# Decoder layer on one core: the down projection as seven 2x2 block products instead of eight

## The chip, the cores and the metric

One Trainium2 chip, of which the program uses a single core. The metric is the device time of one execution in microseconds (us), as the median of several runs. The profile is one further execution, taken by the hardware profiler.

## The reference

One inference step of a decoder layer for 1024 prompt tokens and 8 sample tokens, 1032 in all, in 32-bit floats. Sparse attention, a gated delta rule and a cross-attention over memory come first; the change leaves their code alone. It concerns the last line of the layer, a SwiGLU feed-forward of width 2816 on a model width of 1024:

```python
hf = rmsnorm(x, ffn_norm_g)
x = x + (jax.nn.silu(hf @ w_gate) * (hf @ w_up)) @ w_down
```

## The kernel before

Activations stand transposed: 128 features on the partitions, tokens along the free dimension. So the hidden activations are 22 row blocks of 128 features by 1032 tokens, and the residual `xT` is 8 blocks of 128 by 1032. The tokens are split into a first half of 512 (`HN`) and a second of 520 (the 8 sample tokens stand at its end).

Every product is made to nearly full precision from three matmuls in the faster format (`three`, L1775, and `proj`, L129). Each operand is split into a rounded part `h` and a rest `l`, and TensorE sums h*h, h*l and l*h. For weights `split_w` (L121) does this: a cast on ScalarE (L125) makes `wh`, a subtraction on GpSimd (L126) makes `wl`, with two buffers for each. For activations `split` (L142) does it with a cast on ScalarE (L143) and a subtraction on VectorE (L144).

**Gate and up units.** Eleven calls of `unit_product` (L1812) make two row blocks of the hidden activations each. They already use a 2x2 block scheme: sums of weight blocks (`S`, L1836), split into `sh` and `sl` (L1841, L1842) with seven buffers each, against sums of activations (`T2` to `T4`), in pieces of 260 tokens. One of the four result blocks, the first row block for the first token half, is made by `early` and `first` (L1784, L1801) before the units. In the unit the results are in `uu` (three buffers in all) and `s1`; gate results pass through SiLU on ScalarE, GpSimd multiplies gate and up (L1900), and SP's queue stores the products into a scratch tensor `scrF` in DRAM (L1901).

**Down projection.** `stage_down` (L1940) fetches hidden row blocks from `scrF` (`fetch`, L1934: load `af`, then `split`) in three lots of 8, 7 and 7 blocks, and reloads the residual from `scrT`. `down` (L1903) goes over the 8 output blocks of 128: load the weights (`load_w`, L113), split them, and for each group of tokens (512, 256 and 264, `GROUPS2`) make the product into a PSUM bank `pd`, which VectorE adds to `xT` (L1913). The first lot is done for the group of 512 first and then for the other two groups. With the last lot `store_y` (L1917) transposes each finished output block on TensorE (bank `py`) and stores it.

The order of the instructions on each engine and queue is set by the framework's list scheduler, from the order in the program as priority and from its own estimate of times; on the chip each engine and queue then takes its list in order. Tiles of one tag share a fixed number of buffers, and a tile waits until one is free. Unit tiles (`unit`, tag `u`) have five buffers in this stage.

Of the kernel before, what the change touches and what calls it, by code (L numbers as in the profile page):

```python
# [6 lines left out]
F32 = mybir.dt.float32  # L7
FR = mybir.dt.float32r
BF = mybir.dt.bfloat16
I32 = mybir.dt.int32  # L10
# [3 lines left out]
OP = mybir.AluOpType  # L14
# [25 lines left out]
class Kernel:  # L40
# [111 lines left out]

    def consts(self):
        nc, c = self.nc, self.c
        jp = c.tile([128, 128], I32, name="jp")
# [1645 lines left out]
    def first(self, u, kind, s1, p, sg):  # L1801

        V = self.nc.vector
        if kind == "gate":
            V.tensor_add(sg[:, 0], s1, p)
            self.silu(sg[:, 0], sg[:, 0])
        else:
            V.tensor_add(sg[:, 1], s1, p)  # L1808
            self.nc.gpsimd.tensor_mul(sg[:, 1], sg[:, 0], sg[:, 1])
            self.nc.sync.dma_start(self.scrF[2 * u, :, 0:HN], sg[:, 1])  # L1810

    def unit_product(self, u):  # L1812

        nc, V = self.nc, self.nc.vector
        w = HN + NS
        halves = (slice(0, w // 2), slice(w // 2, w))
# [4 lines left out]
        sg = {}  # L1821
        for kind in ("gate", "up"):
            raw = []
# [22 lines left out]
            t2 = total(t1, a11)  # L1846
            t4 = total(a12, t2)
# [44 lines left out]
            c = [u1, u2[:, :HN], s1]  # L1892
            if kind == "gate":
                for x in c:
                    self.silu(x, x)
                sg["c"] = c
            else:
                f = 2 * u
                for x, y, dst in zip(c, sg["c"], (self.scrF[f, :, HN:], self.scrF[f + 1, :, 0:HN], self.scrF[f + 1, :, HN:])):
                    nc.gpsimd.tensor_mul(x, x, y)  # L1900
                    nc.sync.dma_start(dst, x)  # L1901

    def down(self, f0, acts, groups, last=False):  # L1903
        nc, V = self.nc, self.nc.vector
        kt = len(acts)
        for o in range(KD):
            wh, wl = self.load_w(self.i["w_down"][0][128 * f0:128 * (f0 + kt), 128 * o:128 * o + 128], kt, 128)
            for g in groups:
                g0, n = self.G[g]
                p = self.bank("g", "pd")  # L1910
                self.proj(wh, wl, 0, 128, g, p, kt=kt, act=lambda k: [x[:, g0:g0 + n] for x in acts[k]])
                x = self.xT[:, o, g0:g0 + n]
                V.tensor_add(x, x, p[:, :n])  # L1913
            if last:
                self.store_y(o)

    def store_y(self, o):  # L1917
        nc = self.nc
        cs = slice(128 * o, 128 * o + 128)
        for half in range(2):  # L1920
            p = self.bank("g", "py")
            for t in range(4):
                c = 128 * (4 * half + t)
                self.tr(p[:, 128 * t:128 * t + 128], self.xT[:, o, c:c + 128], 128)
            y = self.unit("y", [128, 4, 128])
            (nc.vector.tensor_copy if half else nc.scalar.copy)(y, p.rearrange("p (t c) -> p t c", c=128))
            nc.sync.dma_start(self.o["y_prompt"][0, 512 * half:512 * half + 512, cs].rearrange("(t p) c -> p t c", p=128), y)
        p = self.bank("g", "py")
        self.tr(p[:NS, :128], self.xT[:, o, T:NT], 128)
        y = self.unit("y8", [NS, 128])  # L1930
        nc.scalar.copy(y, p[:NS, :128])
        nc.scalar.dma_start(self.o["y_sample"].rearrange("b o d -> (b o) d")[:, cs], y)

    def fetch(self, f, h, l, s):  # L1934

        a = self.unit("af")[:, :s.stop - s.start]
        self.nc.sync.dma_start(a, self.scrF[f, :, s])
        self.split(a, h[:, s], l[:, s])

    def stage_down(self, after_units):  # L1940

        acts = [(self.AH[:, k], self.AL[:, k]) for k in range(KD)]
        n1, n2, n = slice(0, HN), slice(HN, NT), slice(0, NT)
        for f in range(8):
            self.fetch(f, *acts[f], n1)
        after_units()
        for o in range(KD):
            self.nc.sync.dma_start(self.xT[:, o, n1], self.scrT[:, o, n1])  # L1948
        for f in range(8):
            self.fetch(f, *acts[f], n2)  # L1950
        self.down(0, acts, (0,))
        for o in range(KD):
            self.nc.sync.dma_start(self.xT[:, o, n2], self.scrT[:, o, n2])
        self.down(0, acts, (1, 2))
        more = [[self.du.tile([128, UW], FR, name="d" + x, tag="d")[:, :NT] for x in "hl"] for _ in range(7)]
        for f in range(8, 15):
            self.fetch(f, *more[f - 8], n)
        self.down(8, more, (0, 1, 2))
        for f in range(15, 22):
            self.fetch(f, *acts[f - 15], n)  # L1960
        self.down(15, acts[:7], (0, 1, 2), True)


    def build(self):
        tc, nc = self.tc, self.nc
        P = tc.alloc_tile_pool
# [5 lines left out]
        self.AH = self.act.tile([128, KD, NT], FR, name="AH")  # L1972
        self.AL = self.act.tile([128, KD, NT], FR, name="AL")
# [55 lines left out]
        self.scrT, self.scrF = self.dr.tile([128, KD, NT], F32, name="scrT"), self.dr.tile([22, 128, NT], F32, name="scrF")  # L2029
# [8 lines left out]
        m = lambda name, shape, dt=FR: self.mkp.tile(shape, dt, name=name)  # L2038
# [13 lines left out]
        def after_units():  # L2052
            for p in (self.tp, self.gw, self.gv):
                p.release()
            self.keep = P(name="keepD", bufs=1)
            self.xT = self.keep.tile([128, KD, NT], F32, name="xT")
            self.du = P(name="du", bufs=14)

        self.stage_down(after_units)
        for p in (self.wp, self.du, self.keep, self.u, self.act, self.c, self.dr, self.ps):  # L2060
            p.release()

    def sample_gen(self):
# [33 lines left out]
```

## Time and profile before

| | |
|---|---|
| median of 3 runs | 1780.9 us (1780.2 to 1784.61) |
| the profiled execution's own time | 1789.59 us |
| its span, first to last instruction | 1787.4 us |
| mean granted clock of TensorE | 0.952 |
| gate and up units in the span | about 1193 to 1513 us |
| down stage in the span | about 1513 us to the end |

TensorE's clock is given as a share of its full 2.4 GHz. Matmuls are pipelined: the duration of one is longer than the distance to the next, so the cost of a matmul is read from the distance of starts. Idle time of an engine is put down to what ended the wait.

### The profile page before, as it was taken

To read this page: it belongs to the slowest core of one execution; us is meant where nothing else is said; L and a number is where in the kernel's file an instruction comes from. 1 tells how busy PE (TensorE), PEld (TensorE's weight loads), DVE (VectorE), ACT (ScalarE), POOL (GpSimd) and SP (SyncE) were. 2 spreads that over 40 slices of the span, in tenths; PEclk is the share of its full clock that TensorE was granted. 3 is DMA by queue.
4 is the path that set the end of the run, shared out by engine and by line. 5 is a ranking of instruction groups with operands and counts; after the bars stand their busy time and mean duration, and the time that the engine had idled before them with its cause. 6 is when DMAs were issued, how large, how long until landed. Compare 5 with 4: busy or idle time off the path is not lost. (4 is left out here: it accounts for less than half of the span.)

```text
span 1787.4 us, 31531 instructions
## 1 busy us (share of the span) xinstructions
PE 1634.5 (91%) x11316; PEld 1442.3 (81%) x11316; DVE 1106.3 (62%) x2913; ACT 880.8 (49%) x2069; POOL 827.7 (46%) x791
## 2 busy tenths in 40 slices
PE   6999988768859999989998899879999999899998
PEld 5989877768747777768896578669999999599998
DVE  7699996999979777762355523775556666313111
ACT  5568879964546666664565564432222323212111
POOL 1277663573147133225553436765656566342210
PEclk9999998879979899979998999989999999999999
DMA  4134354324242324256322244553444444922132
GB/s 156 46 91 130 118 145 125 119 90 134 85 121 63 82 72 122 78 156 184 89 83 59 79 140 148 190 160 101 137 125 126 130 131 132 313 82 86 42 90 58
DMA packets 268630, 206.44 MB, mean 115 GB/s; under 512 B 31397, under 2 KB 240506, under 8 KB 268338
## 3 DMA queue, kind: packets, MB, share of 16 engines
q1 hardware_dynamic: 249674, 175.34, 32.6%
q0 software_dynamic: 4864, 14.69, 2.9%
q10 hardware_dynamic: 13936, 14.40, 2.3%
q8 instruction: 89, 1.46, 0.3%
q14 instruction: 67, 0.55, 0.1%
HBM read 152.01 MB, written 52.47 MB: 114 GB/s over the span
## 5 line engine op out<-in xcount | busy, mean ns | idle before, releaser
L126 POOL TENSOR_TENSOR wl<-raw,wh 128x1024 fp32r<-128x1024 f32 (+2 forms) x107 | 255.3, 2387 | 401.8 <-ACT wh L125 329.0
L48 PE MATMUL pm<-AH,wh 128*128 128x384 f32 (+7 forms) x792 | 269.8, 341 | 4.6 <-ACT y L111 4.0
L48 PE MATMUL pm<-AH,wl 128*128 128x384 f32 (+7 forms) x792 | 263.0, 332 | 0.1
L48 PE MATMUL pm<-AL,wh 128*128 128x384 f32 (+7 forms) x792 | 262.7, 332 | 0.1
L125 ACT CAST wh<-raw 128x1024 fp32r<-128x1024 f32 (+2 forms) x107 | 110.0, 1029 | 255.5 <-PE pd L48 172.4
L48 PEld LDWEIGHTS pm<-AH,wh 128*128 128x128 f32 (+1 forms) x792 | 154.0, 195 | 12.0 <-ACT y L111 4.6
L1842 POOL TENSOR_TENSOR sl<-S,sh 128x512 fp32r<-128x512 f32 x88 | 119.7, 1371 | 89.6 <-ACT sh L1841 86.9
L48 PEld LDWEIGHTS pm<-AL,wh 128*128 128x128 f32 (+1 forms) x792 | 154.0, 194 | 6.7 <-issue 0.8
L48 PEld LDWEIGHTS pm<-AH,wl 128*128 128x128 f32 (+1 forms) x792 | 152.9, 193 | 5.1 <-issue 0.7
L1913 DVE TENSOR_TENSOR xT<-xT,pd 128x256 f32<-128x256 f32 (+2 forms) x72 | 36.8, 512 | 190.5 <-PE pd L48 190.4
L1841 ACT CAST sh<-S 128x512 fp32r<-128x512 f32 x88 | 53.3, 619 | 183.5 <-DVE S L1836 170.6
L48 PE MATMUL pd<-AH,wh 128*128 128x512 f32 (+2 forms) x360 | 116.3, 325 | 5.1 <-ACT wh L125 5.1
L48 PE MATMUL pd<-AH,wl 128*128 128x512 f32 (+2 forms) x360 | 115.4, 322 | 3.7 <-POOL wl L126 3.7
L48 PE MATMUL pd<-AL,wh 128*128 128x512 f32 (+2 forms) x360 | 115.1, 321 | 0.0
L1836 DVE TENSOR_TENSOR S<-raw 128x512 f32<-128x512 f32 x44 | 54.8, 1246 | 92.0 <-DMA raw<-in_w_gate 38.0
L48 PE MATMUL p<-AL,sh 128*128 128x260 f32 x352 | 99.7, 283 | 0.0
L48 PE MATMUL p<-AH,sh 128*128 128x260 f32 x352 | 99.6, 283 | 0.0
L48 PE MATMUL p<-AH,sl 128*128 128x260 f32 x352 | 99.3, 283 | 0.0
L48 PE MATMUL pg<-AH,wh 128*128 128x512 f32 x176 | 73.3, 419 | 14.6 <-DVE sg L1808 7.5
L1866 DVE TENSOR_TENSOR uu<-uu,p 128x260 f32<-128x260 f32 x176 | 71.9, 420 | 16.4 <-PE p L48 14.7
L48 PEld LDWEIGHTS pd<-AH,wh 128*128 128x128 f32 x360 | 68.1, 189 | 11.9 <-ACT wh L125 6.8
L48 PEld LDWEIGHTS pd<-AH,wl 128*128 128x128 f32 x360 | 67.9, 189 | 10.6 <-POOL wl L126 5.3
(703 smaller groups left out, 5153.8 us busy)
## 6 DMA issues: line engine op xcount, KB each, us to landing
raw<-in_w_gate SPq DMA_DIRECT2D x33, 512.0 KB
raw<-in_w_up SPq DMA_DIRECT2D x33, 512.0 KB
raw<-in_w_in SPq DMA_DIRECT2D x24, 512.0 KB
raw<-in_w_out SPq DMA_DIRECT2D x16, 512.0 KB
raw<-in_w_down SPq DMA_DIRECT2D x16, 512.0 KB
af<-scrF SPq DMA_DIRECT2D x14, 516.0 KB
raw<-in_w_down SPq DMA_DIRECT2D x16, 448.0 KB
scrG<-y ACTq DMA_DIRECT2D x32, 192.0 KB
```

Of the source, the lines that this page charges most:

```text
L48: return self.nc.tensor.matmul(out, lhsT, rhs, start=start, stop=stop)
L125: self.nc.scalar.copy(wh, raw)
L126: self.nc.gpsimd.tensor_sub(wl, raw, f32(wh))
L1836: op(t, x, y)
L1841: nc.scalar.copy(h, x)
L1842: nc.gpsimd.tensor_sub(l, x, f32(h))
L1866: V.tensor_add(out[:, c], x[:, c], p[:, :w // 2])
L1913: V.tensor_add(x, x, p[:, :n])
```

## The change

The hidden activations are now four blocks: b11 and b12 (even row blocks, first and second token half), b21 and b22 (odd row blocks). The down weights are four blocks A11, A12, A21, A22: output half by even or odd row blocks, each 512 outputs by 11 row blocks. Instead of eight block products `stage_down` makes seven, of these weights and operands, in this order: A11 with b11 (operand 0), A22 with operand 4, S1 with 1, S2 with 2, S4 with 5, S3 with 3, A12 with b21 (operand 6). Only A11's and A12's are 512 tokens wide; the others have 520, in two pieces of 260.

The operands' sums are made in the units by a new function `down_blocks` and stored in a scratch tensor `scrD`. The weights' sums stay in one buffer `S`, which each product turns into the next: S1 = A22 + A21, S2 = S1 - A11, S4 = A12 - S2, S3 = A11 - A21 (this one loads two blocks). Weights come in pieces of six and five row blocks per output block. A sum `U` collects what goes into several results. Operands of the next product are fetched two per step during the current one, into the other half of `AH` and `AL` or into six buffers `du`; the residual is reloaded piecemeal in the first three products. `store_y` now stores one token half at a time. Other edits: `AH` and `AL` are 1040 instead of 1032 wide, and the index tile `jp` moves to the pool of unit tiles. The core of the diff:

```diff
-            self.nc.sync.dma_start(self.scrF[2 * u, :, 0:HN], sg[:, 1])
+            self.nc.sync.dma_start(self.scrD[0, u, :, :HN], sg[:, 1])
...
             if kind == "gate":
...
+                b11 = self.unit("b11", [128, HN])
+                nc.sync.dma_start(b11, self.scrD[0, u, :, :HN])
             else:
-                f = 2 * u
-                for x, y, dst in zip(c, sg["c"], (self.scrF[f, :, HN:], self.scrF[f + 1, :, 0:HN], self.scrF[f + 1, :, HN:])):
-                    nc.gpsimd.tensor_mul(x, x, y)
-                    nc.sync.dma_start(dst, x)
+                self.down_blocks(u, b11, (u1, u2, s1), sg["c"])
+    def down_blocks(self, u, b11, up, gate):
+        nc, G, V = self.nc, self.nc.gpsimd, self.nc.vector
+        (b12, b21, b22), (t3, t4, t2) = up, gate
+        store = lambda j, x: nc.sync.dma_start(self.scrD[j, u, :, :x.shape[-1]], x)
+        G.tensor_mul(b12, b12, t3)
+        G.tensor_mul(b22, b22, t2)
+        G.tensor_mul(b21[:, :HN], b21[:, :HN], t4[:, :HN])
+        store(5, b22)
+        store(6, b21[:, :HN])
+        V.tensor_sub(t3, b22, b12)
+        store(3, t3)
+        V.tensor_sub(b12[:, :HN], b12[:, :HN], b11)
+        store(1, b12)
+        G.tensor_sub(t2, b22, b12)
+        store(2, t2)
+        V.tensor_sub(t4[:, :HN], b21[:, :HN], t2[:, :HN])
+        V.tensor_scalar(t4[:, HN:], t2[:, HN:], -1.0, None, op0=OP.mult)
+        store(4, t4)
...
     def stage_down(self, after_units):
...
+        order = ((0, HN, "A11"), (4, w, "A22"), (1, w, "S1"), (2, w, "S2"), (5, w, "S4"), (3, w, "S3"), (6, HN, "A12"))
+        W = self.i["w_down"][0].rearrange("(u two p) c -> two p u c", two=2, p=128)
...
+        def weights(name, m, ks):
+            t = S[:, m, ks]
+            get = lambda i, j: block(i, j, m, ks, self.wd, 3)
+            if name in ("A11", "A12"):
+                return self.split_w(block(1, int(name[2]), m, ks, self.wp, 2))
+            if name == "A22":
+                nc.sync.dma_start(t, W[1][:, ks, 512 + 128 * m:512 + 128 * m + 128])
+            elif name == "S1":
+                V.tensor_add(t, t, get(2, 1))
+            elif name == "S2":
+                V.tensor_sub(t, t, get(1, 1))
+            elif name == "S4":
+                V.tensor_sub(t, get(1, 2), t)
+            else:
+                V.tensor_sub(t, get(1, 1), get(2, 1))
+            return self.split_w(t)
+        def finish(name, m, banks):
...
+            if name == "A11":
+                nc.scalar.copy(u[:, :HN], banks[0])
+            elif name == "S1":
+                add(c22)
+                add(c12)
+            elif name == "S2":
+                add(u)
+                G.tensor_add(c12, c12, u)
+            elif name == "S4":
+                add(c12)
+                return [(m, 1)]
+            elif name == "S3":
+                add(u)
+                V.tensor_add(c22, c22, u)
+                G.tensor_add(c21, c21, u[:, :HN])
+                return [(m + 4, 1), (m + 4, 0)]
+            elif name == "A22":
+                add(c21)
+                G.tensor_add(c11, c11, u[:, :HN])
+            else:
+                add(c11)
+                return [(m, 0)]
...
+        for q, (_, n, name) in enumerate(order):
+            more = (fetches(q + 1, range(11)) if q < 6 else iter(()), residual(*back.get(q, ())))
+            halves = (slice(0, HN),) if n == HN else (slice(0, w // 2), slice(w // 2, w))
+            for m in range(4):
+                banks = [self.bank("g", "pd") for _ in halves]
+                for ks in (slice(0, 6), slice(6, 11)):
+                    wh, wl = weights(name, m, ks)
+                    for p, c in zip(banks, halves):
+                        for k in range(ks.start, ks.stop):
+                            h, l = slots[q][k]
+                            self.three(p[:, :c.stop - c.start], wh[:, k - ks.start], wl[:, k - ks.start], h[:, c], l[:, c], k == 0, k == 10)
+                    for g in (more[1], more[0], more[0]):
+                        next(g, None)
+                    store()
+                done += finish(name, m, banks)
...
+            self.du = P(name="du", bufs=6, side="right")
             self.keep = P(name="keepD", bufs=1)
             self.xT = self.keep.tile([128, KD, NT], F32, name="xT")
-            self.du = P(name="du", bufs=14)
+            self.U = self.keep.tile([128, 4, HN + NS], F32, name="U")
+            self.S = self.keep.tile([128, 4, 11, 128], F32, name="Sd")
+            self.wd = P(name="wd", bufs=1)
```

## Rows read from the trace of the kernel before

**Rows 1.** The page, busy time of each engine, share of the span, instructions.

```profile
PE 1634.5 (91%) x11316; PEld 1442.3 (81%) x11316; DVE 1106.3 (62%) x2913; ACT 880.8 (49%) x2069; POOL 827.7 (46%) x791
```

**Rows 2.** Windows: us, busy (x) of PE, PEld, DVE, ACT, POOL; clock; DMA share, GB/s.

```profile
1193.40:1512.80 319.40, 318.36 (x2632) 318.03 (x2633) 187.33 (x356) 89.73 (x155) 191.30 (x141) 0.99 0.41 126
1512.80:1557.30 44.50, 35.75 (x148) 26.79 (x146) 20.32 (x23) 15.74 (x17) 16.10 (x8) 1.00 0.92 321
1557.30:1705.00 147.70, 147.69 (x999) 136.88 (x1000) 31.37 (x52) 24.82 (x26) 43.61 (x20) 0.99 0.25 74
```

**Rows 3.** The chain that ended last: start us, us, what.

```profile
1262.45 214.59 PE p L48 x1788
...
1557.31 147.64 PE pd L48 x997
1704.95 1.07 PE py L51 x9
...
1771.81 9.90 PE pd L48 x63
1781.71 0.97 PE py L51 x8
```

**Rows 4.** Timeline of TensorE, down stage: start us, duration us, instruction, idle before and releaser.

```profile
1524.98 0.50 PE L48 MATMUL pd<-AH,wh 128*128 128x512 f32 x1 [0.84 <-ACT wh L125]
...
1527.53 0.50 PE L48 MATMUL pd<-AH,wl 128*128 128x512 f32 x1 [1.81 <-POOL wl L126]
...
1645.40 0.39 PE L48 MATMUL pd<-dh,wh 128*128 128x512 f32 x1
...
1650.26 0.28 PE L48 MATMUL pd<-dh,wh 128*128 128x256 f32 x1
```

**Rows 5.** Groups by form, 1512 us to the end: busy us, mean ns, idle before.

```profile
L126 POOL TENSOR_TENSOR wl<-raw,wh 128x896 fp32r<-128x896 f32 x16 | 34.1, 2132 | 121.0 <-ACT wh L125 77.8 <-PE py L51 43.2
L126 POOL TENSOR_TENSOR wl<-raw,wh 128x1024 fp32r<-128x1024 f32 x14 | 33.6, 2402 | 55.9 <-ACT wh L125 55.9
L1913 DVE TENSOR_TENSOR xT<-xT,pd 128x512 f32<-128x512 f32 x24 | 16.4, 686 | 95.0 <-PE pd L48 95.0
L125 ACT CAST wh<-raw 128x896 fp32r<-128x896 f32 x16 | 15.1, 941 | 126.9 <-PE pd L48 126.9
L125 ACT CAST wh<-raw 128x1024 fp32r<-128x1024 f32 x14 | 14.7, 1049 | 59.9 <-PE pd L48 45.6 <-DMA raw<-in_w_down 14.3
L1913 DVE TENSOR_TENSOR xT<-xT,pd 128x264 f32<-128x264 f32 x24 | 10.3, 429 | 48.7 <-PE pd L48 48.6
```

**Rows 6.** Windows as in rows 2: one of weight loads alone, one with full DMA engines.

```profile
1660.00:1670.00 10.00, 10.00 (x65) 9.08 (x64) 1.54 (x3) 0.94 (x1) 2.12 (x1) 1.00 0.16 47
1530.00:1540.00 10.00, 8.91 (x38) 6.58 (x37) 7.55 (x7) 3.90 (x4) 2.60 (x2) 1.00 1.07 375
```

**Rows 7.** Timeline of ScalarE in the entry of the down stage.

```profile
1521.71 1.05 ACT L143 CAST dh<-af 128x1032 fp32r<-128x1032 f32 x1 [3.52 <-DMA af<-scrF]
...
1523.89 1.04 ACT L125 CAST wh<-raw 128x1024 fp32r<-128x1024 f32 x1
```

**Rows 8.** Waits, 1512 us to the end: us in total, times, longest us.

```profile
ACT AH L143 <- DMA af<-scrF: 7.1, 5, 4.4
```

**Rows 9.** Timelines of GpSimd and VectorE in a unit.

```profile
1463.25 1.31 POOL L1900 TENSOR_TENSOR uu<-uu 128x520 f32<-128x520 f32 x1
1464.52 3.00 POOL L1842 TENSOR_TENSOR sl<-S,sh 128x512 fp32r<-128x512 f32 x2
...
1475.77 2.55 POOL L1842 TENSOR_TENSOR sl<-S,sh 128x512 fp32r<-128x512 f32 x2 [5.75 <-ACT sh L1841]
...
1459.25 0.69 DVE L1836 TENSOR_TENSOR S<-S,raw 128x512 f32<-128x512 f32 x1
...
1463.32 1.79 DVE L1836 TENSOR_TENSOR S<-raw 128x512 f32<-128x512 f32 x1 [1.77 <-POOL sl L1842]
```

**Rows 10.** Waits of TensorE, 1193 to 1512.8 us, the longest in total.

```profile
PE p L48 <- POOL sl L1842: 1.6, 1, 1.6
```

More of the change, by code (lines that the diff above doesn't have):

```diff
@@ L154, in consts @@
         nc, c = self.nc, self.c
-        jp = c.tile([128, 128], I32, name="jp")
+        jp = self.unit("jp", [128, 128], I32)
         nc.gpsimd.iota(jp, pattern=[[1, 128]], base=0, channel_multiplier=-1)
@@ L1891, in unit_product @@
             plus(u1, u1, product(4, "B22", "p3"))
-            c = [u1, u2[:, :HN], s1]
             if kind == "gate":
-                for x in c:
+                for x in (u1, u2[:, :HN], s1):
                     self.silu(x, x)
-                sg["c"] = c
-            else:
-                f = 2 * u
-                for x, y, dst in zip(c, sg["c"], (self.scrF[f, :, HN:], self.scrF[f + 1, :, 0:HN], self.scrF[f + 1, :, HN:])):
-                    nc.gpsimd.tensor_mul(x, x, y)
-                    nc.sync.dma_start(dst, x)
@@ L1903, in down @@
[L1903 to L1915, printed above, removed]
@@ L1917, in store_y @@
-    def store_y(self, o):
+                sg["c"] = u1, u2, s1
+                b11 = self.unit("b11", [128, HN])
+                nc.sync.dma_start(b11, self.scrD[0, u, :, :HN])
+            else:
+                self.down_blocks(u, b11, (u1, u2, s1), sg["c"])
[17 more added lines that the diff above has]
+        store(4, t4)
@@ L1918, in store_y @@
+    def store_y(self, o, half):
         nc = self.nc
         cs = slice(128 * o, 128 * o + 128)
-        for half in range(2):
-            p = self.bank("g", "py")
[L1922 to L1938, printed above, removed]
-    def stage_down(self, after_units):
[L1942 to L1945, printed above, removed]
-        after_units()
[L1947 to L1961, printed above, removed]
@@ new lines, in store_y @@
+        p = self.bank("g", "py")
+        for t in range(4):
+            c = 128 * (4 * half + t)
+            self.tr(p[:, 128 * t:128 * t + 128], self.xT[:, o, c:c + 128], 128)
+        y = self.unit("y", [128, 4, 128])
+        nc.scalar.copy(y, p.rearrange("p (t c) -> p t c", c=128))
+        nc.sync.dma_start(self.o["y_prompt"][0, 512 * half:512 * half + 512, cs].rearrange("(t p) c -> p t c", p=128), y)
+        if half:
+            p = self.bank("g", "py")
+            self.tr(p[:NS, :128], self.xT[:, o, T:NT], 128)
+            y = self.unit("y8", [NS, 128])
+            nc.scalar.copy(y, p[:NS, :128])
+            nc.scalar.dma_start(self.o["y_sample"].rearrange("b o d -> (b o) d")[:, cs], y)
@@ new lines, in fetch, with slot, fetches, residual @@
+    def fetch(self, j, u, h, l):
+        a = self.unit("af")[:, :h.shape[-1]]
+        self.nc.sync.dma_start(a, self.scrD[j, u, :, :h.shape[-1]])
+        self.split(a, h, l)
+    def stage_down(self, after_units):
+        nc, V, G = self.nc, self.nc.vector, self.nc.gpsimd
+        w = HN + NS
+        order = ((0, HN, "A11"), (4, w, "A22"), (1, w, "S1"), (2, w, "S2"), (5, w, "S4"), (3, w, "S3"), (6, HN, "A12"))
+        W = self.i["w_down"][0].rearrange("(u two p) c -> two p u c", two=2, p=128)
+        n1, n2 = slice(0, HN), slice(HN, NT)
+        def slot(q, u):
+            n = order[q][1]
+            if u < KD:
+                return [t[:, u, w * (q % 2):w * (q % 2) + n] for t in (self.AH, self.AL)]
+            t = self.du.tile([128, 2, w], FR, name="d", tag="d")
+            return [t[:, i, :n] for i in range(2)]
+        def fetches(q, us):
+            for u in us:
+                slots[q].append(slot(q, u))
+                self.fetch(order[q][0], u, *slots[q][u])
+                yield
+        slots = [[] for _ in order]
+        for _ in fetches(0, range(8)):
+            pass
+        after_units()
+        for _ in fetches(0, range(8, 11)):
+            pass
+        x, U, S = self.xT, self.U, self.S
+        def residual(*tiles):
+            for o, s in tiles:
+                nc.sync.dma_start(x[:, o, s], self.scrT[:, o, s])
+                yield
+        back = {0: [(4, n1), (5, n1)], 1: [(6, n1), (0, n1), (7, n1), (1, n1), (2, n1), (3, n1), (4, n2), (0, n2)],
+                2: [(5, n2), (1, n2), (6, n2), (2, n2), (7, n2), (3, n2)]}
+        G.memset(U[:, :, HN:], 0.0)
+        def block(i, j, m, ks, pool, bufs):
+            t = pool.tile([128, ks.stop - ks.start, 128], F32, name="raw", tag="raw", bufs=bufs)
+            nc.sync.dma_start(t, W[j - 1][:, ks, 512 * (i - 1) + 128 * m:512 * (i - 1) + 128 * m + 128])
+            return t
+        def weights(name, m, ks):
[15 more added lines that the diff above has]
+        def finish(name, m, banks):
+            def add(out):
+                for p, c in zip(banks, halves):
+                    c = slice(c.start, min(c.stop, out.shape[-1]))
+                    V.tensor_add(out[:, c], out[:, c], p[:, :c.stop - c.start])
+            c11, c12, c21, c22 = x[:, m, n1], x[:, m, n2], x[:, m + 4, n1], x[:, m + 4, n2]
+            u = U[:, m]
+            if name == "A11":
[20 more added lines that the diff above has]
+                return [(m, 0)]
+            return []
+        done = []
+        def store():
+            while done:
+                self.store_y(*done.pop(0))
+        for q, (_, n, name) in enumerate(order):
[5 more added lines that the diff above has]
+                    wh, wl = weights(name, m, ks)
+                    for p, c in zip(banks, halves):
+                        for k in range(ks.start, ks.stop):
[5 more added lines that the diff above has]
+                done += finish(name, m, banks)
+        store()
@@ L1971, in build @@
         self.act = P(name="act", bufs=1)
-        self.AH = self.act.tile([128, KD, NT], FR, name="AH")
-        self.AL = self.act.tile([128, KD, NT], FR, name="AL")
+        self.AH = self.act.tile([128, KD, UW], FR, name="AH")
+        self.AL = self.act.tile([128, KD, UW], FR, name="AL")
         self.keep = P(name="keep", bufs=1)
@@ L2028, in build @@
         self.u = P(name="uB", bufs=5)
-        self.scrT, self.scrF = self.dr.tile([128, KD, NT], F32, name="scrT"), self.dr.tile([22, 128, NT], F32, name="scrF")
+        self.scrT, self.scrD = self.dr.tile([128, KD, NT], F32, name="scrT"), self.dr.tile([7, 11, 128, HN + NS], F32, name="scrD")
         self.E, self.scrS = 0, self.dr.tile([11, 128, 2, HN + NS], F32, name="scrS")
@@ L2054, in after_units @@
                 p.release()
+            self.du = P(name="du", bufs=6, side="right")
             self.keep = P(name="keepD", bufs=1)
             self.xT = self.keep.tile([128, KD, NT], F32, name="xT")
-            self.du = P(name="du", bufs=14)
+            self.U = self.keep.tile([128, 4, HN + NS], F32, name="U")
+            self.S = self.keep.tile([128, 4, 11, 128], F32, name="Sd")
+            self.wd = P(name="wd", bufs=1)
         self.stage_down(after_units)
-        for p in (self.wp, self.du, self.keep, self.u, self.act, self.c, self.dr, self.ps):
+        for p in (self.du, self.wp, self.wd, self.keep, self.u, self.act, self.c, self.dr, self.ps):
             p.release()
```

## The prediction, made before the run

> **What bounds the kernel now.** I read the page's busy shares first: TensorE is busy 91% of the span, the others 46 to 62% [rows 1]. A share is an average, so the next view is the table of windows from the gate and up units on [rows 2]. In the units (1193.4 to 1512.8) TensorE works 318.36 of 319.40 us at full granted clock, VectorE 59%, GpSimd 60%. The down stage that the change rewrites has three parts. In its entry (1512.8 to 1557.3) TensorE is busy only 35.75 of 44.50 us while the DMA engines stand at 0.92; after 1557.3 TensorE is solid and DMA falls to about a quarter. The chain of waits says the same: from 1557.31 one unbroken piece of `pd` matmuls, then `py` transposes and `pd` in turn up to 1781.71, and a short drain [rows 3]. So in the down stage the time is matmul time, except in the entry.
>
> What the entry loses: all 1584 `pd` matmuls are 192 each of 512, 256 and 264 columns for the first eight row blocks and 168 each twice for the rest. Of these, 997 + 7x63 come after 1557.31, so 146 of 512 columns lie in the entry. A 512-column matmul takes (1650.26-1645.40)/21 = 0.2314 us [rows 4], 146 of them 33.8 us; the entry lost 44.5-33.8 = 10.7 us. The 997 after it, counted the same way, are 145.7 us of work in 147.64: 1.9 us more. Together **12.6 us**.
>
> **Matmul work.** Before: seven row blocks cost 9.90 us for 63 matmuls [rows 3], so one set of 512+256+264 costs 0.471 us; 528 sets are 248.7 us. After: seven products of 11 row blocks, 4 output blocks and 3 terms, 132 matmuls each per column piece. A11 and A12 take one piece of 512 (264 matmuls x 0.2314 = 61.1 us). The other five take two pieces of 260, which the units already run: 214.59/1788 = 0.1200 us [rows 3]; 1320 x 0.1200 = 158.4 us. Sum 219.5 us, **29.2 us less**. The number of matmuls stays 1584; the columns fall by an eighth. The 72 transposes stay, seven at 1.07 and one at 0.97 us [rows 3]. The drain gains a 512-column add in place of a 264-column one, about 0.26 us more [rows 5]: 0.3.
>
> If nothing stalled, the gain would be 29.2+12.6-0.3 = 41.5 us. Now what it may cost.
>
> **Entry.** Before, fifteen operand loads (eight second halves, seven `more`) and sixteen residual loads went out at once. After, product A11 needs eleven 512-column operands, of which eight come during the units as before; the residual is spread over three products; the weights come in pieces of six and five blocks. Still the first residual load goes into memory of the last unit's `uu`, which is now kept until operand 4 is stored, three dependent operations later; on SP it blocks the weight loads behind it. Entry traffic, from the shapes: A11's weights 2.9 MB, A22's operands 2.9, its first weights about 1, late operands 0.8, last unit's stores 1.6, residual 0.5: 9.7 MB in 30.6 us, 317 GB/s. A full stretch moved 375, weight loads alone 47/0.16 = 294 [rows 6]: the DMA engines are nearly full here again. Between 0 and 12.6 us lost; I take the middle, **6**.
>
> **Later products: the splits.** Each step needs a weight piece rounded by ScalarE and its rest made by GpSimd, with two buffers each, so both must be done in one step of TensorE. From the two forms shown [rows 5] the slopes are 0.84 and 2.11 ns a column: six blocks (768) cost 0.83+1.86 = 2.69 us beside a five-block step of 30x0.120 = 3.60; five blocks 0.73+1.59 = 2.32 beside 4.32. The cover is 0.9 and 2.0 us. What can eat it:
> - ScalarE takes its queue in order, and now 66 operand casts (0.63 us) stand among the weight casts, 11 a product up to A12's. Before, this happened once plainly: a `dh` cast waited 3.52 us for its load, the `wh` cast came at 1523.89, and TensorE lost 0.84+1.81 us [rows 4, 7]. Operand loads that ScalarE waited for waited 7.1/5 = 1.4 us each [rows 8]. Bounds: nothing (no such loss after 1557), or one event of 2.65 us twice a product, 32 us. I take one wait of 1.4 us per product, **8.4**, nearest to the wait row, since five load buffers run ahead.
> - VectorE and GpSimd. A sum that reads two SBUF operands takes 0.69 us alone and 1.79 when GpSimd has started first: it began at 1463.32, GpSimd's multiplication held until 1464.56, it ended 0.55 us later, and GpSimd's next pair took 3.00 us, where such a pair takes 2.55 undisturbed [rows 9]. So these operations exclude each other, VectorE's holding about 0.55 us. By that, S2 needs 4x(1.86+1.59) = 13.8 us of splits, four adds of 1.31, eleven operand subtractions of 0.55, and four weight sums of 1408 columns at 1408/512x0.55 = 1.5: 13.8+5.2+6.1+6.0 = 31.1 us, of 31.7 that TensorE needs. S3 comes to 33 with its extra add, S1 and S4 to 26, A22 to 25: 141 of 158. It fits on the sum, barely in two products. Bounds: nothing, or 0.9 us on each of 24 output blocks, 22. I take 0.2 each, **4.8**.
>
> The Trainium skill, page "SBUF — State Buffer", section "Who interferes with whom", says that a VectorE instruction with two SBUF inputs and a GpSimd one that reads SBUF exclude each other and the second to start fully blocks. The trace agrees, 1.79 for 0.69 us. It speaks against this change, which adds such work on both sides: by the rule taken strictly the sum would be the third rival's 1775 us, by my reading of the sum of the holds 1760.5.
>
> VectorE's own sum stays under: S1 has four adds of about 0.42 us per output block. Weight sums run ahead: S of one product may be overwritten once the former's split is done. S3 loads two blocks per step through three buffers; with 5.8 MB of weights at 294 GB/s, 2.8 of operands at 375 and the first outputs it needs nearly all of its 31.7 us of DMA if nothing ran ahead. Over the whole stage 23.1 MB of weights and 20.4 of operands are 79+54 us, and 8.4 MB of residual and outputs 22 to 29: about 160 of 230.
>
> **Units.** Per unit, three subtractions on VectorE and one on GpSimd more (3x0.69+1.31 us), and on SP three more stores and one load. The multiplication order and stores are otherwise the old ones. `uu`, with three buffers, is held longer, and SP's stores for sums stand before later weight loads. TensorE waited for GpSimd 1.6 us once in all of the units [rows 10], with seven buffers of split sums ahead. Cost between 0 and the whole 3.4 us in each of 11 units, 37; I take **2**, by that row. The early corner units only change the address of a store.
>
> **Sum.** 41.5-6-8.4-4.8-2 = 20.3 us. The profiled execution took 1789.59 us (span 1787.4), 8.7 above the median 1780.9; I take the difference over: 1780.9-20.3, rounded, **1760.5 us**. About 0.3% (5.3 us) is what a measurement of this kernel can tell from no change.
>
> **Rivals.**
> 1. No stall to speak of: the cover holds everywhere and the entry is clean. 1780.9-41.5 = 1739.4. For it: TensorE's solid 147 us with casts in it; against: DMA goes from a quarter to over two thirds. 10%.
> 2. Slower: the splits become the bound. With cast, fetch cast (0.63), GpSimd add (1.31) and one VectorE hold all ahead of each rest, an output block's two splits take 0.83+0.73+2x0.63+1.86+1.59+1.31+2x0.55 = 8.7 us against 7.92, and with one 1.4 us load wait at each 10.1: 2.2 us on 24 blocks is 52, and 6 in the entry: 1780.9-41.5+58 = 1797. It decides from 1.7 us per output block (28 blocks) on. Against: the pieces need not follow each other, since ScalarE works on the next while GpSimd does the last. 13%.
> 3. The shared access of VectorE and GpSimd binds: the exclusion costs 0.6 us per output block beyond my sum: 1775. 11%.
> 4. The units lose their cover: `uu` held until operand 4 is stored, and later weight loads behind SP's waits. 2 us a unit: 1780. Against: TensorE's one wait of 1.6 us for a split there [rows 10]. 10%.
> 5. The forecast, 1744 to 1774: 56%.
>
> **Numbers.** The range 1740 to 1783 holds the forecast, rivals 3 and 4, and reaches to the edge of 1; what it leaves out is 2 and about half of 1. Faster: 0.54 of the forecast, all of 1 and nearly all of 3, a little of 4: 0.76. Same: most of 4 and the edges of 3: 0.10. Slower: rival 2 and a rest of 4: 0.14.
>
> **What would show it.** Right: 264 `pd` matmuls of 512 columns and 1320 of 260, at 0.231 and 0.120 us; units still about 319 us; a down stage of 250 to 260 us against 274.6; TensorE's idle time before `pd` mostly put down to `wh` and `wl`. Wrong: over 330 us of units; gaps of over 1.7 us at every output block; `pd` waiting for VectorE's operand rests at product borders, which my sum holds at nothing because operands are fetched two steps ahead of need; a granted clock under 1 between products.

## The result and the profile after

The changed kernel took 1806.84 us in the median of four runs (1802.45 to 1810.62), the kernel before 1780.55 beside it (1779.73 to 1784.61): ratio 1.0129, interval 1.0107 to 1.0151. It is **slower** by 26.3 us, and the time lies outside the predicted range. The profiled execution took 1810.62 us with a span of 1808.6, against a span of 1787.4 before: 21.2 us more, which the traces have to explain. These two executions lie 9.0 (before) and 3.8 us (after) above their medians, so the traces show 5 us less than the medians do, and a few us between two profiles need not come from the change.

The page's busy shares answer to [rows 1]. TensorE does 8.7 us less work in a span 21 us longer; VectorE's work grows by 110 us and GpSimd's by 67.

```profile
PE 1625.8 (90%) x11316; PEld 1441.8 (80%) x11316; DVE 1216.5 (67%) x3012; ACT 921.8 (51%) x2152; POOL 894.8 (49%) x839
```

The next view is the windows, which answer to [rows 2]. First the kernel before, all of its units from the first matmul on (1190.6), with the columns of [rows 2]:

```profile
1190.60:1512.80 322.20, 319.58 (x2640) 319.03 (x2641) 187.73 (x357) 90.10 (x156) 194.10 (x143) 0.99 0.42 127
```

The changed kernel: its units, then the seven products A11, A22, S1, S2, S4, S3 and A12 with the drain:

```profile
1179.90:1547.40 367.50, 333.61 (x2640) 331.03 (x2641) 239.24 (x398) 89.55 (x155) 215.69 (x155) 0.95 0.45 139
1547.40:1590.40 43.00, 35.20 (x135) 26.14 (x134) 19.97 (x24) 15.88 (x25) 19.28 (x13) 0.93 1.06 335
1590.40:1622.70 32.30, 32.30 (x266) 32.07 (x265) 19.62 (x26) 13.69 (x21) 14.93 (x9) 0.99 0.80 246
1622.70:1655.20 32.50, 32.08 (x267) 31.79 (x265) 24.44 (x34) 12.16 (x19) 15.14 (x9) 1.00 0.62 182
1655.20:1687.30 32.10, 31.89 (x267) 31.68 (x266) 23.47 (x27) 12.17 (x19) 19.91 (x12) 1.00 0.60 172
1687.30:1734.50 47.20, 39.18 (x282) 37.47 (x281) 21.24 (x26) 12.54 (x22) 16.39 (x10) 0.89 0.58 165
1734.50:1770.00 35.50, 35.37 (x299) 35.08 (x298) 15.66 (x20) 15.64 (x28) 19.34 (x11) 1.00 0.37 109
1770.00:1808.60 38.60, 33.70 (x159) 27.08 (x157) 3.88 (x6) 8.98 (x14) 13.55 (x8) 0.97 0.34 96
```

Three parts can be read off. **Before the units** the changed kernel is 10.7 us ahead (1179.9 against 1190.6). **The units** take 367.5 instead of 322.2 us: 45.3 lost. **The down stage** takes 261.2 instead of 274.6: 13.4 gained. Sum +21.2. The units' row says more: the same 2640 matmuls, but idle time is 33.9 us where it was 2.6 (31.3 more), and busy time 333.6 where it was 319.6 (14.0 more) at a granted clock of 0.95 instead of 0.99. So the units lose by gaps and by a lower clock together.

**What the gaps are.** The waits of 1193 to 1530 us answer to [rows 10]; instead of one wait of 1.6 us for GpSimd there is now VectorE's `uu` (total, times, longest):

```profile
PE p L48 <- DVE uu L1866: 26.7, 10, 3.8
```

L1866 is the addition that takes a result out of a PSUM bank. The bank of tag `g` that TensorE wants next is free only after it, and there are eight. The timeline of one unit shows why it is late (start, duration, engine; idle before and releaser in brackets):

```profile
1383.43 0.41 DVE L1866 TENSOR_TENSOR uu<-s,p 128x260 f32<-128x260 f32 x1
1383.77 1.45 DVE L1912 TENSOR_TENSOR uu<-s,uu 128x520 f32<-128x520 f32 x1
1385.15 0.41 DVE L1866 TENSOR_TENSOR uu<-s,p 128x260 f32<-128x260 f32 x1
1385.48 1.44 DVE L1914 TENSOR_TENSOR uu<-uu,b 128x512 f32<-128x512 f32 x1
1388.41 1.73 DVE L1918 TENSOR_TENSOR uu<-uu,s 128x512 f32<-128x512 f32 x1 [1.48 <-POOL s L1916]
1390.06 1.23 DVE L1919 TENSOR_SCALAR uu<-s 128x8 f32<-128x8 f32 x1
1391.20 0.87 DVE L1866 TENSOR_TENSOR uu<-uu,p 128x260 f32<-128x260 f32 x2
...
1387.07 1.31 POOL L1916 TENSOR_TENSOR s<-s,uu 128x520 f32<-128x520 f32 x1 [0.70 <-PE p L48]
1388.33 1.26 POOL L1842 TENSOR_TENSOR sl<-raw,sh 128x512 fp32r<-128x512 f32 x1
1389.55 1.71 POOL L1842 TENSOR_TENSOR sl<-S,sh 128x512 fp32r<-128x512 f32 x1
...
1388.13 0.28 PE L48 MATMUL p<-AH,sl 128*128 128x260 f32 x1
1391.76 0.36 PE L48 MATMUL p<-T2h,sh 128*128 128x260 f32 x1 [3.35 <-DVE uu L1866]
```

Between 1385.56 and 1391.20 VectorE empties no bank: it does the unit's operand sums (L1914, L1918, L1919), and in the midst of them waits 1.48 us for the sum that GpSimd makes. TensorE fills what banks there are until 1388.4 and then stands 3.35 us. The chain that [rows 3] showed as one unbroken piece of `p` matmuls now runs through these sums (start, us, what):

```profile
1387.10 1.29 POOL s L1916
1388.38 0.02 issue
1388.41 1.73 DVE uu L1918
1390.14 1.15 DVE uu L1919
1391.29 0.34 DVE uu L1866
```

After the gap the clock is low: windows of the stretch before, right after and further on.

```profile
1386.00:1391.70 5.70, 2.42 (x21) 2.21 (x19) 4.18 (x5) 0.00 (x0) 4.56 (x4) 1.00 0.71 229
1391.70:1395.00 3.30, 3.24 (x19) 3.27 (x20) 2.14 (x6) 0.64 (x1) 0.00 (x0) 0.68 0.74 203
1395.00:1400.00 5.00, 5.00 (x39) 5.00 (x38) 2.99 (x6) 2.28 (x4) 1.20 (x1) 0.87 0.34 131
```

0.68 is a mean over both levels (1.2 and 2.4 GHz). The timeline has eleven gaps ahead of a T2 product that end with L1866, of 1.7 to 5.4 us, 32.1 in all. With the six of 3.2 to 5.4 us the clock fell like this, with the five of 1.7 to 2.4 it stayed at full. Nine of the eleven follow a unit's sums as shown. The gap at 1507.32 does not: there VectorE stands 5.75 us at the rest of an operand that the down stage fetches early (L144) and whose load is late, with the additions behind it:

```profile
1506.14 0.69 DVE L144 TENSOR_TENSOR AL<-af,AH 128x512 fp32r<-128x512 f32 x1 [5.75 <-ACT AH L143]
...
1507.32 0.56 PE L48 MATMUL p<-T2h,sh 128*128 128x260 f32 x1 [3.81 <-DVE uu L1866]
```

The last and longest gap (5.42 us, at 1530.29) has both ahead of it, such rests and the sums.

**The down stage.** Matmul work is as predicted (264 of 512 columns and 1320 of 260 at the same spacings, 219.5 us). What each product lost beyond its `pd` and `py` matmuls, counted from starts: A11 12.9 us, A22 0.2, S1 0.8, S2 0.3, S4 13.7, S3 0.0, A12 with the drain 5.1. A11 stands with the DMA engines full (1.06, 335 GB/s, as [rows 6]). S4 doesn't: its DMA share is 0.58. By the windows above 7.8 us of A11's loss and 8.0 of S4's are idle time; the rest is slower matmuls, at a mean granted clock of 0.93 and 0.89. The timelines in S4 of SP, ScalarE, VectorE and TensorE:

```profile
1690.69 16.03 SPq L1987 DMA_DIRECT2D raw<-in_w_down  x8
1706.77 0.99 SPq L1943 DMA_DIRECT2D af<-scrD  x2
...
1711.88 0.62 ACT L143 CAST AH<-af 128x520 fp32r<-128x520 f32 x1 [9.12 <-DMA af<-scrD]
1712.41 0.72 ACT L125 CAST wh<-Sd 128x640 fp32r<-128x640 f32 x1
...
1712.53 0.70 DVE L144 TENSOR_TENSOR AL<-af,AH 128x520 fp32r<-128x520 f32 x1 [1.98 <-ACT AH L143]
1713.15 0.42 DVE L2011 TENSOR_TENSOR xT<-xT,pd 128x260 f32<-128x260 f32 x1
...
1713.62 0.83 PE L51 MATMUL py<-ident,xT 128*128 128x128 f32 x3 [3.23 <-DVE xT L2011]
...
1726.81 0.39 PE L48 MATMUL pd<-AH,wh 128*128 128x260 f32 x1 [2.44 <-ACT wh L125]
```

SP spends 16 us on eight weight loads for S3, which needs two blocks per step, because it has to wait for the three load buffers: it issues each pair as VectorE's subtraction of the pair before ends. The operand loads behind them go out at 1706.77. ScalarE stands 9.12 us at an operand cast with the weight cast behind it, VectorE stands at the rest of the same operand with the addition to `xT` behind it, and TensorE stands 3.23 us at the transposes that need `xT`, later 2.44 us for weights. Over the down stage (1547 us to the end) the wait that was 7.1 us in 5 times [rows 8] is now, for the operands in `AH` and for those in the buffers `du`:

```profile
ACT AH L143 <- DMA af<-scrD: 29.3, 13, 9.1
...
ACT d L143 <- DMA af<-scrD: 20.3, 11, 7.2
```

### The profile page after: what moved, and what is told of

Its sections match the earlier page's. It is cut to its first block, busy times and chain, and to the rows that moved or that the text cites. A ratio compares the mean times of both kernels' runs of the same rounds, so it can differ in the third digit from the quotient of the medians.

```text
span 1808.6 us, 32094 instructions
## 1 busy us (share of the span) xinstructions
PE 1625.8 (90%) x11316; PEld 1441.8 (80%) x11316; DVE 1216.5 (67%) x3012; ACT 921.8 (51%) x2152; POOL 894.8 (49%) x839
## 5 line engine op out<-in xcount | busy, mean ns | idle before, releaser
L126 POOL TENSOR_TENSOR wl<-raw,wh 128x1024 fp32r<-128x1024 f32 (+2 forms) x91 | 210.7, 2317 | 236.9 <-ACT wh L125 207.5
L1842 POOL TENSOR_TENSOR sl<-S,sh 128x512 fp32r<-128x512 f32 x88 | 125.9, 1441 | 95.6 <-ACT sh L1841 95.6
L125 ACT CAST wh<-raw 128x1024 fp32r<-128x1024 f32 (+2 forms) x91 | 90.5, 996 | 88.1 <-PE pd L48 23.1
L48 PE MATMUL pd<-AH,wh 128*128 128x260 f32 (+1 forms) x384 | 116.5, 307 | 7.1 <-ACT wh L125 7.1
L48 PE MATMUL pd<-AH,wl 128*128 128x260 f32 (+1 forms) x384 | 115.9, 310 | 5.8 <-POOL wl L126 5.7
L48 PE MATMUL pd<-AL,wh 128*128 128x260 f32 (+1 forms) x384 | 115.5, 305 | 0.0
L126 POOL TENSOR_TENSOR wl<-Sd,wh 128x768 fp32r<-128x768 f32 (+1 forms) x40 | 74.0, 1851 | 83.2 <-ACT wh L125 79.3
L48 PE MATMUL p<-T2h,sh 128*128 128x260 f32 x176 | 56.3, 320 | 35.0 <-DVE uu L1866 32.1
L48 PEld LDWEIGHTS pd<-AH,wh 128*128 128x128 f32 x384 | 73.3, 191 | 11.7 <-ACT wh L125 9.1
L48 PEld LDWEIGHTS pd<-AH,wl 128*128 128x128 f32 x384 | 72.1, 191 | 11.3 <-POOL wl L126 8.6
```

What stands on the lines that cost most here:

```text
L48: return self.nc.tensor.matmul(out, lhsT, rhs, start=start, stop=stop)
L125: self.nc.scalar.copy(wh, raw)
L126: self.nc.gpsimd.tensor_sub(wl, raw, f32(wh))
L1842: nc.gpsimd.tensor_sub(l, x, f32(h))
```

## The experiments

Theory: the units lose because the operand sums stand in VectorE's order ahead of the additions that free PSUM banks; S4 loses because of SP's order. Rivals: the work itself (the sharing of VectorE and GpSimd, the stores) costs the time wherever it stands; the rest of the change (the down stage's buffers, the layout) does it.

**The sums later.** `down_blocks` ends after `store(6, ...)`; the sums and their stores are put out in the next gate unit, behind the addition after which `s1` is complete (the last unit does them at once).

```diff
-            plus(s1, u2, p5)
+            last = plus(s1, u2, p5)
+            if kind == "gate" and u:
+                with self.tc.issue_after(last.ins):
+                    self.later()
```

> The same instructions as in the changed kernel; the four VectorE sums of a unit (and the GpSimd one between them) are only queued behind the adds that empty the banks of the next unit's third and second product. Theory (VectorE takes the sums ahead of the adds that free PSUM banks, and TensorE waits for a bank): the eleven gaps of TensorE at the start of a unit's third product (T2), 35 us in all, go to under 8, the units take 322 to 332 us instead of 367.5, and the whole 1765 to 1775. Rival (the added work itself, and the exclusion between VectorE and GpSimd): the gaps move elsewhere, units over 350 us, whole within 8 us of 1807. Second rival (the buffer uu is held too long): the sums now end later still, so the gaps grow; over 1815.

1778.34 us in the median of 10 runs, before 1781.29; ratio 0.9986 (0.9971 to 1.0001). Units 336.3 us. TensorE's groups at the T2 product (busy, mean ns, idle before and releaser), first in the changed kernel, 1193 to 1547 us:

```profile
L48 PE MATMUL p<-T2h,sh 128*128 128x260 f32 x168 | 53.2, 317 | 32.1 <-DVE uu L1866 32.1
```

Then in this kernel, whole units:

```profile
L48 PE MATMUL p<-T2h,sh 128*128 128x260 f32 x176 | 50.7, 288 | 5.3 <-ACT sh L1841 2.9 <-DVE uu L1866 2.4
L48 PE MATMUL p<-T4h,sh 128*128 128x260 f32 x176 | 50.6, 288 | 7.8 <-DVE uu L1866 7.8
```

With the same operations in another place the units take 31 us less: the theory holds for most of the loss. Of the 5.3 us left at T2, 2.9 stand ahead of the first unit, as in the kernel before, and a gap of 2.2 (1503.1) is of the other kind, behind a late operand of the down stage. But the place changes more than what stands behind the sums: VectorE's four take 48.5 us in all instead of 59.8 (from 1193 us on), and its wait of 13.1 us for GpSimd's sum is gone. How the 31 us divide between these and the order was not separated. Smaller gaps come up at the T4 product, the units stay 4 us over the upper end that was expected and the whole 3 us over. By its time this kernel can't be told from the kernel before.

**The sums on GpSimd.** They stay where they were, but all four run on GpSimd, with the eight columns as part of one subtraction from a cleared tile.

```diff
-        V.tensor_sub(t3, b22, b12)
+        G.memset(b21[:, HN:], 0.0)
+        G.tensor_sub(t3, b22, b12)
...
-        V.tensor_sub(t4[:, :HN], b21[:, :HN], t2[:, :HN])
-        V.tensor_scalar(t4[:, HN:], t2[:, HN:], -1.0, None, op0=OP.mult)
+        G.tensor_sub(t4, b21, t2)
```

> All four sums of a unit go to GpSimd, the eight-column negation is replaced by a subtraction over all 520 columns from cleared columns. Theory (VectorE's queue): VectorE has no more to do than before, so the T2 gaps go; units 322 to 332 us, whole 1765 to 1775. Rival (exclusion and GpSimd's load): GpSimd goes from 60 to over 70% busy in the units and its splits come late; new waits of TensorE for sl, units over 345 us, whole over 1785.

1774.93 us (before 1781.29), ratio 0.997 (0.9954 to 0.9986). The whole is the theory's number, the units, 343.0, are nearly the rival's. T2 gaps are 8.3 us: 2.9 ahead of the first unit, as in the kernel before, and 5.4 in two gaps (1490.1 and 1509.4) behind late operands of the down stage; none follows a unit's sums. So taking the sums off VectorE's queue ends those gaps. GpSimd is busy 247 us in the units instead of 216, 72% as the rival said, but after 1193 us no wait of TensorE for `sl` shows, only waits for VectorE's additions (13.8 us in 17 times at `uu`). What holds these up was not traced.

**The sums alone.** The kernel before, with `down_blocks` and all its stores added to the units and the old stores to `scrF` kept; the old down stage. The sums' results are not used.

```diff
+                self.down_blocks(u, b11, (u1, u2, s1), sg["c"])
...
+        nc.sync.dma_start(self.scrF[f, :, HN:], b12)
```

> The kernel before, with the sums of the units and their stores added, and the old down stage, which does not read them. Theory: the units cost what they cost in the changed kernel, 40 to 50 us more than before, and the down stage is that of before, 270 to 276 us: whole about 1820 to 1830. Rival (the loss in the units comes from the new down stage's early loads on SP): units lose under 15 us, whole under 1800.

1841.22 us in one run. Units 379.0, down stage 275.4: the loss of the units comes with the sums and their stores alone and needs nothing of the new down stage. It is larger than expected, 57 us in the units for 40 to 50 and 11 us over the expected whole; this kernel also stores the products twice, so its size can't be set against that of the changed kernel.

**The layout alone.** The kernel before with the changed places of tiles only.

```diff
-        jp = c.tile([128, 128], I32, name="jp")
+        jp = self.unit("jp", [128, 128], I32)
...
-        self.AH = self.act.tile([128, KD, NT], FR, name="AH")
+        self.AH = self.act.tile([128, KD, UW], FR, name="AH")
```

> The kernel before with only the two small edits: the index tile jp among the unit tiles, AH and AL 1040 columns wide. Theory (the 10.7 us by which the units begin earlier in the changed kernel come from these, through the order that the scheduler then finds for the early stages): units begin at 1178 to 1186 us, whole 1766 to 1774. Rival (it is chance of one execution, or comes from elsewhere): no difference beyond 5 us.

1773.67 us against 1781.29, ratio 0.9946 (0.9924 to 0.9968): 7.6 us faster by the medians, 9.6 by the ratio. The units (321.3 us) and the down stage (274.4) are as before; the gain lies ahead of the units, which begin at 1177.2.

**`jp` alone.** Only the first of these two edits.

> The kernel before with one edit: the 128x128 index tile jp of the constants lies in the pool of the unit tiles instead of the pool of the constants; AH and AL keep 1032 columns. Theory (the order in which the early stages' instructions are put out follows from where the tiles lie, and this tile is made ahead of all of them): the early stages end by 1177 to 1181 us as in x4_layout_alone, units about 322, down stage about 274, whole 1772 to 1777. Rival (the eight further columns of AH and AL, whose tiles stand ahead of all others, shift the rest): the early stages end at 1188 to 1192 and the whole is 1779 to 1783.

1776.64 us against 1783.2, ratio 0.9954 (0.9934 to 0.9974): as much as both, within the intervals. The units begin at 1183.3 in its profile, between the two expected stretches; the profiled execution, 1780.33 us, was the slowest of six. So moving one index tile of 128x128, which no step of the prediction priced, is worth 6.6 us by the medians, 8 by the ratio, in the early stages. By windows of 150 us, TensorE is busy 3.7 us more from 300 to 450 and 8 us more from 450 to 600 than before; which instruction there is earlier was not traced.

**S3's weights with one buffer less.** S3's first block goes straight into `S`, so each step needs one load buffer instead of two.

```diff
-                V.tensor_sub(t, get(1, 1), get(2, 1))
+                nc.sync.dma_start(t, W[0][:, ks, 128 * m:128 * m + 128])
+                V.tensor_sub(t, t, get(2, 1))
```

> Only product S3's weights: A11's block is loaded straight into the sum's buffer and A21's subtracted from it, so that one load buffer of three is used per step instead of two; as many bytes. Theory (the 13.7 us lost in product S4 come from SP standing 16 us on S3's weight loads for a free load buffer, with S3's operand loads queued behind, and ScalarE, in order, waiting up to 9.1 us for these with weight casts behind): S4 loses under 4 us, units as in the changed kernel (360 to 370 us), whole 1792 to 1802. Rival (S4 and S3 have too many bytes for the DMA engines): S4's loss stays over 9 us or moves into S3, whole 1803 to 1812.

1801.39 us in one run. S4 loses 6.7 us instead of 13.7: half. SP's order was a cause, but not the whole: the whole time came as expected, "under 4" was missed.

**Later, and half on GpSimd.** As the sums later, with operand 4 made by GpSimd (`G.memset` and one `G.tensor_sub`).

> The later-queued sums of the first experiment, with the last of them (operand 4) on GpSimd over 520 columns, so that VectorE makes two sums per unit, waits for GpSimd in none and makes no eight-column negation. Theory (what is left in the units there, 336 against 322 us, is VectorE's wait for GpSimd's sum and the negation of about 1.2 us, again ahead of adds that free banks): units 324 to 331 us, whole 1766 to 1774. Rival (what is left is the exclusion, work for work): units 334 to 340, whole 1776 to 1782.

1765.51 us in one run, units 335.1: the rival's number for the units, though the whole is under both ranges. No better than leaving operand 4 with VectorE; the whole is lower by an earlier start of the units (1174.4) and an entry that loses 7.2.

**Both.** The kernel of the run before with S3's edit.

> The two edits before together. If the causes are separate the gains add: units 324 to 331 us, S4 loses under 4 us, down stage 246 to 252 us, whole 1756 to 1768 (faster than the kernel before by 0.8 to 1.4%). Rival of bytes: as the run before it, 1766 to 1776.

1764.88 us against 1780.44, ratio 0.9918 (0.9888 to 0.9948): **faster than the kernel before by 0.8%**, and under the changed kernel's 1806.84. The whole and the down stage (249.3) came as expected; the units, 339.9 for 324 to 331, and S4, about 7 us for under 4, did not. Its entry, S4 and S3, columns as above:

```profile
1512.70:1549.80 37.10, 31.93 (x133) 23.84 (x132) 21.09 (x23) 17.69 (x28) 20.55 (x15) 1.00 1.00 317
1646.80:1687.00 40.20, 35.17 (x280) 33.41 (x280) 18.08 (x23) 11.51 (x20) 16.94 (x10) 1.00 0.61 178
1687.00:1722.90 35.90, 35.54 (x298) 35.04 (x297) 18.12 (x25) 16.85 (x30) 18.95 (x11) 1.00 0.43 126
```

**The entry's order.** `x7_both` with A22's weight loads held until A11's last weight load is out, and each residual load behind the latest weight load.

```diff
+                with self.tc.issue_after(self.load.ins):
+                    nc.sync.dma_start(x[:, o, s], self.scrT[:, o, s])
...
+                with self.tc.issue_after(self.first_loads):
+                    nc.sync.dma_start(t, W[1][:, ks, 512 + 128 * m:512 + 128 * m + 128])
```

> As the run before, and on SP's queue A22's weight loads are put behind the last weight load of A11, each residual load behind the weight load traced last before it. Theory (the entry's 7 to 15 us come from loads needed later, issued early, that share full DMA engines with A11's weights): A11 loses 2 to 6 us, whole 1750 to 1764. Rival (the entry is bound by the bytes it needs anyway): A11 loses as much as before or A22 begins to lose; no gain.

1764.65 us, ratio 0.9908 (0.9882 to 0.9933): as `x7_both`. A11 loses 8.2 us, not less, at a DMA share of 0.98, and the whole misses its range by 0.65 us: the rival. Putting A22's weights and the residual later doesn't help here; A22's operand loads stayed where they were.

**Output transposes later.** `x7_both` with S4's transposes one weight block further back in TensorE's order.

> x7_both, and in product S4 alone the transposes of a finished output tile are put one weight block further back in TensorE's order. Theory (what S4 still loses, 6.8 us in x7_both, is TensorE standing at these transposes, 1.75, 0.77 and shorter ones, for the xT addition, which stands behind the weights' subtraction in VectorE's queue, itself waiting up to 6.0 us for the transfer into Sd): S4 loses 2 to 4 us, the down stage is 245 to 247, the whole 1759 to 1763. Rival (the stall moves on to the next weight halves, which are late by themselves): S4 loses 5.5 to 7.5 and the whole is as x7_both, 1763 to 1767.

1768.92 us against 1783.2, ratio 0.9903 (0.9874 to 0.9932): as `x7_both`. S4 loses 7.4 us: the rival. TensorE's longest waits are now for weights (1.35, 1.15 and 1.12 us). ScalarE's timeline says why:

```profile
1682.91 1.33 ACT L143 CAST d<-af 128x520 fp32r<-128x520 f32 x2 [6.96 <-DMA af<-scrD]
1684.15 0.83 ACT L125 CAST wh<-Sd 128x768 fp32r<-128x768 f32 x1
```

A weight cast is again behind an operand cast that waited for its load.

## Why the prediction was wrong

The predicted change was -20.3 us, the profiles show +21.2. The 41.5 us between them, by the prediction's own parts: units +43.3 (45.3 for 2), down stage +8.9 (261.2 for 252.3, which is 274.6-29.2-12.6+0.3+6+8.4+4.8), early stages -10.7 (for 0).

- **Units: the step that failed.** "Cost between 0 and the whole 3.4 us in each of 11 units, 37; I take 2, by that row" chose its value from a wait of TensorE for GpSimd [rows 10]. The added sums were measured against their engines' totals, not against what stood behind them in VectorE's order: the additions that free PSUM banks. It named what stands behind SP's waits and not what stands behind VectorE's sums. `x1_sums_later` and `x2_sums_on_gpsimd` show that it is this: with the sums behind the additions, or off VectorE, no T2 gap follows them, and the units lose 14 and 21 us instead of 45. Nor did the upper end hold, for two reasons. A sum counted at 0.69 us takes 1.44 to 1.80, and the eight columns, counted at nothing, 1.23 (groups of VectorE in the changed kernel, 1193 to 1547 us, below); and the lower clock after the gaps makes the same matmuls 14.0 us longer.

```profile
L1918 DVE TENSOR_TENSOR uu<-uu,s 128x512 f32<-128x512 f32 x10 | 18.0, 1802 | 13.1 <-POOL s L1916 13.1
...
L1912 DVE TENSOR_TENSOR uu<-s,uu 128x520 f32<-128x520 f32 x10 | 15.2, 1521 | 0.0
...
L1914 DVE TENSOR_TENSOR uu<-uu,b 128x512 f32<-128x512 f32 x10 | 14.4, 1440 | 0.0
L1919 DVE TENSOR_SCALAR uu<-s 128x8 f32<-128x8 f32 x10 | 12.2, 1225 | 0.0
```

- **The exclusion** of VectorE and GpSimd was seen [rows 9] but only charged as 0.55 us of GpSimd's time per operation. What it costs VectorE, the rest of a GpSimd instruction each time, was left out. The reading in the down stage, 4.8 us, fell on nothing that can be seen: S1, S2 and S3 lost 0.8, 0.3 and 0.0. The third rival, by which the page "SBUF — State Buffer" of the Trainium skill, section "Who interferes with whom" (the second to start is blocked for the whole instruction of the first), costs time there, had the rule right and the place wrong. The trace agrees with the rule in the units: L1918 starts at 1388.41, ends 0.55 us after GpSimd's split ended at 1389.59.
- **Matmul work** -29.2: right, in counts, forms and spacings.
- **Entry** at 6: it lost 12.9 with the DMA engines at 1.06, just over the upper end of its bounds; this is 6.9 of the down stage's 8.9. It doesn't hang on the two orders that `x8_entry_order` changed. It was 12.4 and 15.2 in `x5_s3_into_s` and `x1_sums_later` and about 7 to 8 in the five kernels where GpSimd makes operand 4; why that helps here was not traced.
- **Splits behind ScalarE's order** at 8.4: the mechanism was right in part, the distribution was not. Not one wait of 1.4 us per product but under 1 us lost in each of A22, S1, S2 and S3 and 13.7 us in S4, where SP's order made operand loads up to 9.12 us late. "Five load buffers run ahead" is true only while SP issues their loads; the three buffers of S3's weights stopped it. TensorE's waits for weights in S4 (2.44 and 1.11 us) go by the predicted mechanism; the longest, 3.23, goes by VectorE's order, where the addition to `xT` stands behind a late operand's rest, and that was held at nothing. That the total is near (15.0 lost in the five middle products, 13.2 predicted for both terms) is luck.
- **Rival 2**, the only one slower than before (1797), put the loss into the down stage's splits; that stage gained 13.4 us. **Rival 4** named the place, the units, but another mechanism (`uu` held, SP's waits) and 2 us a unit. TensorE's waits in the units show none on a store of `uu`, and in `x1_sums_later`, where the sums end later still, the gaps close. Loads that are late do show, as the down stage's operands in the last two gaps.
- **Early stages** at 0: the layout edit was treated as no cost, and gives back 6.6 and 7.6 us by the medians of the two runs of it, 8 to 10 by the ratios. The rest of the 10.7 can be the two profiled executions, which lie 9.0 and 3.8 us over their medians; in `x3_sums_alone`, without the edit, the units begin at 1185.1 and not at 1190.6. Without the layout edit, by the sum of the two, the change would be 33 to 36 us slower; that wasn't run.
- Of the signs the prediction gave for being wrong, "over 330 us of units" and "a granted clock under 1" are what came.

What stays open: the units of the best kernel are still some 18 us over 322, with gaps of 0.4 to 2.1 us at VectorE's additions; about 7 us each are left in A11 and S4. And of the 15.6 us that `x7_both` gains by the medians (14.6 by the ratio), 6.6 to 7.6 (8 to 10 by the ratios) are the layout's, if the two add. So the seven products would bring some 5 to 9 us more than the operands' sums cost.

## What to carry to other kernels

Work that is added to an engine with spare time is not priced by its busy time: look at what stands behind it in that engine's order, above all the instructions that free PSUM banks, and put it behind those. Next to a stream of GpSimd work an SBUF operation of VectorE can cost the rest of a GpSimd instruction, however small it is itself. A queue that loads for two products stops for the scarcer buffer, and everything behind it is late, though the DMA engines stand at 0.58, as in S4 here.

## What the runs showed of the hardware

An eight-column operation on VectorE took 0.16 us where GpSimd was idle and 1.23 beside its splits. First all eleven L1919 of the changed kernel (min/median/max in ns):

```profile
L1919 DVE TENSOR_SCALAR uu<-s x11: 158/1225/1229, 1228.3 to 1555.8; 128x8 f32<-128x8 f32 x11
```

Then the shortest, on the timelines of VectorE and GpSimd, whose split had ended at 1555.29:

```profile
1555.77 0.16 DVE L1919 TENSOR_SCALAR uu<-s 128x8 f32<-128x8 f32 x1
...
1553.45 1.84 POOL L126 TENSOR_TENSOR wl<-raw,wh 128x768 fp32r<-128x768 f32 x1
1556.67 1.90 POOL L126 TENSOR_TENSOR wl<-raw,wh 128x640 fp32r<-128x640 f32 x1 [1.37 <-ACT wh L125]
```

By the timeline of one unit above, L1919 starts at 1390.06 and ends when GpSimd's split does.

The other: after TensorE's gap of 3.35 us the granted clock was a mean of 0.68 in the next 3.3 us and 0.87 in the five after, though TensorE then worked without a break; the gaps' price in the units was 31.3 us of idle time and 14.0 of slower matmuls.
